# A two-layer attention and ffn block on one core: seams between stages, head, and who makes the low parts

## The chip, the cores and the metric
One core of a Trainium2 chip runs the whole program. The metric is the device time of one execution in microseconds (us); the time given for a kernel is the median of its runs.

## The reference, cut to what matters
Two layers, each a gated attention mixer and a convolutional ffn, with an rms norm ahead of each part and the residual added behind it (512 tokens, width 1024, float32):

```python
for l in range(2):
    h = rms_norm(x, g_pre_mix[l])
    m = hybrid_mixer(h, positions, w_in[l], ...)   # q, k, v, gates = h @ w_in; rope; two attentions
    x = x + rms_norm(m, g_post_mix[l])             # m = (g_a * (o_nsa @ w_a) + g_b * (o_sb @ w_b)) @ w_out
    h = rms_norm(x, g_pre_ffn[l])
    f = conv_ffn(h, w_up[l], conv_w[l], conv_b[l], w_down[l])
    x = x + rms_norm(f, g_post_ffn[l])
```

## The kernel before, in words
Everything lies feature-major, [128, 8, 512] for width 1024. The weights stream through three raw buffers `wraw` in chunks of 512 KB, by transfers on SyncE's queue (L73), in the order of a list made at the start. ScalarE casts a chunk to its high part `whi` (L94), and VectorE (DVE) or GpSimd, as the list says, subtracts it to get the low part `wlo` (L95); both have two buffers. Chunks that are kept for six tiles have both parts in one tile, `wh`. A projection (`gemm`, L362) makes three matmuls for each of the eight feature tiles of a chunk: `h_hi` with `whi`, `h_lo` with `whi`, `h_hi` with `wlo`.

The norm isn't applied to h. `chain` makes h = x * gain in two parts (`h_hi` on ScalarE, L431, `h_lo` on DVE, L432), and sums the squares of x (ScalarE L435, GpSimd L439); a matmul with ones (L445) sums them over the features, and `rstd_of` (ScalarE L213 and L401, DVE L402 to L404) makes `r2` = 1 / rms, which multiplies the projection later. Ahead of that, when a part has ended, the chain adds the normed part to x: another matmul with ones (L415) on `acc` (mixer) or `f_acc` (ffn), the sums of squares of the part that GpSimd gathers tile by tile (L455).

So that TensorE has work at the seam between two parts, tokens are done by halves. The last tiles of a part run the second half while the chain of the first half runs as a side job; then `head_first` runs the first six tiles (`HEAD`) of the next projection on the first half, beside the chain of the second half, and `head_second` runs them on the second half. At the start of the program the chain has no part to add, and position tables (`rt_...`, sine and cosine, written to memory and read back as `cs_t`) are made beside `head_first`.

Behind the first six tiles of the mixer's input projection (`w_m`) come three chunks of `w_vn` (840, 840 and 560 columns, values, token-major), and `w_m` chunks 6 and 7. Key and query tiles are rotated on the way: a copy `rf`, its halves swapped by four transfers into `rs`, DVE products with `cs_t`. The rotated `kd` goes by transfers to `cstk`, which the matmuls of L671 read. The ffn's down projection `w_d` comes in pieces of 1024, 1024 and 768 columns for each output tile; the last three tiles (`TAIL_D`) are done by halves.

A scheduler with a cost model decides in which order each engine gets its instructions; each engine then runs its own in that order, and waits for the others by semaphores.

## Time and profile before

| | |
|---|---|
| time, median of 3 runs (lowest, highest) | 1701.48 us (1700.77, 1703.69) |
| span of the profiled execution | 1701.4 us |
| TensorE matmul busy (PE) | 1637.3 us, 96% |
| VectorE busy (DVE) | 1114.8 us, 66% |
| ScalarE busy (ACT) | 820.6 us, 48% |
| GpSimd busy (POOL) | 404.8 us, 24% |

The span is the time from the first to the last instruction of one execution, the one that was profiled; what lies around it is within the difference between the three runs. PE is TensorE's matmul stream, PEld its weight loads, which run beside it. An idle time in the timeline stands behind a row in brackets, with what ended it.

### The profile page before, as it was taken

Reading aid. Unit: us, or ns where it says so; the run is one execution under the profiler, and the core shown is the slowest. Engines: PE = TensorE matmul, PEld = TensorE weight load, DVE = VectorE, ACT = ScalarE, POOL = GpSimd, SP = SyncE. Lnnn points to the kernel's source line nnn. Section 1 sums busy time; section 2 is a strip of 40 time slices with the busy share of each in tenths; the row PEclk is TensorE's granted clock in tenths of the full one; section 3 lists DMA queues with packets and bytes.
Section 4 is the critical chain, followed back from the end, with each engine's and each line's share of the span. In section 5 each row is a group of like instructions: output and inputs, shape, how many; then the busy total and the mean of one; then the engine's idle time right before and its main releaser. Section 6 shows DMA issues by size and latency. Waiting matters only on the chain.

```text
span 1701.4 us, 23429 instructions
## 1 busy us (share of the span) xinstructions
PE 1637.3 (96%) x9010; PEld 1401.9 (82%) x9010; DVE 1114.8 (66%) x1595; ACT 820.6 (48%) x1358; POOL 404.8 (24%) x385
## 2 busy tenths in 40 slices
PE   7989999999989999999999999999999999999997
PEld 6878887778988888888888788877889988888896
DVE  8677665766478777722657667577675787776236
ACT  5445564545554444433544555464545454444233
POOL 4125453440240000001331354444203200000011
PEclk9999999999999999999999999999999999999998
DMA  4721112113312333233655211121142223333344
GB/s 163 194 88 50 50 38 63 50 52 135 124 63 75 99 99 98 88 99 102 186 171 146 68 50 51 38 62 50 50 163 85 75 87 99 100 98 91 97 126 138
DMA packets 56800, 159.98 MB, mean 94 GB/s; under 512 B 6512, under 2 KB 18288, under 8 KB 56432
## 3 DMA queue, kind: packets, MB, share of 16 engines
q1 hardware_dynamic: 51984, 147.92, 27.9%
q10 hardware_dynamic: 3552, 6.37, 1.1%
q0 software_dynamic: 1152, 4.19, 0.7%
q8 instruction: 71, 1.16, 0.3%
q14 instruction: 41, 0.34, 0.1%
HBM read 144.82 MB, written 4.72 MB: 88 GB/s over the span
## 4 chain that ended last, share of the span: by engine, by line
PE 82%; DVE 9%; ACT 4%; issue 2%; DMA 2%; POOL 1%; SPq 0%; ACTq 0%; DVEq 0%; POOLq 0%
PE bk L362 52%; PE f L362 16%; PE Z L362 4%; PE pv L362 3%; PE S L362 2%; PE tp L867 2%; DVE rs L425 1%; DVE x L426 1%; PE bk L671 1%; DMA cs_t<-rot 1%; DVE wlo L95 1%; DVE h_lo L432 1%; ACT whi L94 1%; ACT L220 0%; ACT gate L213 0%
## 5 line engine op out<-in xcount | busy, mean ns | idle before, releaser
L94 ACT CAST whi<-wraw 128x1024 fp32r<-128x1024 f32 (+3 forms) x241 | 246.2, 1022 | 351.8 <-PE bk L362 259.3
L95 DVE TENSOR_TENSOR wlo<-wraw,whi 128x1024 fp32r<-128x1024 f32 (+4 forms) x184 | 217.2, 1181 | 217.6 <-ACT whi L94 215.4
L362 PE MATMUL bk<-h_hi,whi 128*128 128x512 f32 (+1 forms) x768 | 288.6, 377 | 12.6 <-ACT whi L94 11.0
L362 PE MATMUL bk<-h_lo,whi 128*128 128x512 f32 (+1 forms) x768 | 290.2, 378 | 3.3 <-DVE h_lo L432 3.2
L362 PE MATMUL bk<-h_hi,wlo 128*128 128x512 f32 (+1 forms) x768 | 289.1, 377 | 4.1 <-DVE wlo L95 4.1
L95 POOL TENSOR_TENSOR wlo<-wraw,whi 128x1024 fp32r<-128x1024 f32 x57 | 141.3, 2480 | 231.2 <-ACT whi L94 187.2
L362 PE MATMUL f<-h_hi,whi 128*128 128x512 f32 x448 | 183.2, 409 | 4.8 <-DVE gate L734 2.0
L455 POOL TENSOR_TENSOR f_acc<-f_acc,sqm 128x256 f32<-128x256 f32 (+1 forms) x19 | 29.1, 1531 | 635.9 <-ACT sqm L454 635.8
L362 PEld LDWEIGHTS bk<-h_hi,whi 128*128 128x128 f32 x768 | 147.8, 193 | 37.6 <-ACT whi L94 11.0
L362 PE MATMUL f<-h_hi,wlo 128*128 128x512 f32 x448 | 178.7, 399 | 0.0
L362 PE MATMUL f<-h_lo,whi 128*128 128x512 f32 x448 | 178.5, 398 | 0.0
L362 PEld LDWEIGHTS bk<-h_hi,wlo 128*128 128x128 f32 x768 | 148.2, 193 | 30.5 <-DVE wlo L95 5.3
L362 PEld LDWEIGHTS bk<-h_lo,whi 128*128 128x128 f32 x768 | 148.3, 193 | 30.0 <-DVE h_lo L432 4.5
L362 PE MATMUL bk<-ah,wlo 128*128 128x256 f32 (+1 forms) x484 | 162.8, 336 | 4.0 <-DVE wlo L95 4.0
L362 PE MATMUL bk<-ah,whi 128*128 128x256 f32 (+1 forms) x484 | 161.1, 333 | 0.0
L362 PE MATMUL bk<-al,whi 128*128 128x256 f32 (+1 forms) x484 | 160.9, 332 | 0.0
L362 PEld LDWEIGHTS f<-h_hi,whi 128*128 128x128 f32 x448 | 85.7, 191 | 25.0 <-DVE sbz L713 4.1
L362 PEld LDWEIGHTS bk<-ah,wlo 128*128 128x128 f32 x484 | 92.5, 191 | 14.2 <-DVE wlo L95 5.0
L856 POOL TENSOR_TENSOR P<-P,st 128x256 f32<-128x256 f32 (+3 forms) x64 | 80.9, 1265 | 82.3 <-DVE st L854 53.1
L1150 DVE TENSOR_TENSOR cu<-bk,r 128x512 f32<-128x512 f32 x88 | 60.1, 686 | 61.2 <-PE bk L362 61.0
L362 PEld LDWEIGHTS f<-h_hi,wlo 128*128 128x128 f32 x448 | 85.5, 191 | 17.7
L362 PEld LDWEIGHTS bk<-ah,whi 128*128 128x128 f32 x484 | 92.6, 191 | 8.8
(227 smaller groups left out, 3456.5 us busy)
## 6 DMA issues: line engine op xcount, KB each, us to landing
wraw<-in_w_u SPq DMA_DIRECT2D x88, 512.0 KB, 3.5
wraw<-in_w_m SPq DMA_DIRECT2D x72, 512.0 KB, 3.3
wraw<-in_w_d SPq DMA_DIRECT2D x44, 512.0 KB, 3.5
wraw<-in_w_d SPq DMA_DIRECT2D x22, 384.0 KB, 3.1
wraw<-in_w_pr SPq DMA_DIRECT2D x16, 512.0 KB, 3.6
wraw<-in_w_o SPq DMA_DIRECT2D x16, 512.0 KB, 3.6
rs<-rf SPq DMA_DIRECT2D x56, 64.0 KB, 3.6
x<-in_xT ACTq DMA_DIRECT2D x4, 512.0 KB, 10.4
```

What stands on the lines that cost most here:

```text
L94: self.nc.scalar.copy(hi[:, c], raw[:, c])
L95: eng.tensor_sub(lo[:, c], raw[:, c], hi.bitcast(F)[:, c])
L362: nc.tensor.matmul(o, a, b, start=first, stop=last, skip_group_check=True)
L425: eng.tensor_mul(t, mt(k), r)
L426: eng.tensor_add(xk, xk, t)
L432: nc.vector.scalar_tensor_tensor(h_lo[:, k, tr], xk, g, h_hi.bitcast(F)[:, k, tr], op0=OP.mult, op1=OP.subtract)
L455: nc.gpsimd.tensor_add(acc, acc, q)
L671: nc.tensor.matmul(cps[v][:64, :65], cw[:, v * 1024 + s * 64:v * 1024 + s * 64 + 64], cstk[:, v, s:s + 513:8], start=(s == 0), stop=(s == 15))
L856: nc.gpsimd.tensor_mul(pv, pv, st[:, None, 2:4, None].to_broadcast([128, self.i + 1, 2, 128]))
L867: nc.tensor.transpose(tp[:, b * 128:(b + 1) * 128], self.P[:, (c + b) * 128:(c + b + 1) * 128], ident)
L1150: nc.vector.tensor_mul(u, b, r2)
```

## The change
It has five parts. (1) At the head x is transferred by SyncE, in four contiguous parts between the first weight chunks (x is kept by token halves, [128, 2, 8, 256]), the first `vec` by ScalarE's queue, and 48 matmuls of a constant tile run first on TensorE. (2) Where the chain has no part to add, the squares come behind all the h's. (3) The matmul on the sum of squares of the first half (`r2_of`) isn't issued at the end of the chain but after the third tile (`LATE` = 2) of `head_first`, and the last sum goes into `r2` itself. (4) The low parts of the second and third `w_vn` chunk, of `w_m` chunks 6 and 7, and of the second piece of the last three second-half `w_d` tiles are made on GpSimd, in both layers. (5) Comments are gone, so that lines are numbered anew.

```diff
-            it(w_vn[l, :, c:c + n], n)
-        it(w_m[l, 6])
-        it(w_m[l, 7])
+            it(w_vn[l, :, c:c + n], n, eng=nc.gpsimd if c else nc.vector)
+        it(w_m[l, 6], eng=nc.gpsimd)
+        it(w_m[l, 7], eng=nc.gpsimd)
...
-        for i in dts:
+        for j, i in enumerate(dts):
             k0 = 0
             for n in DCH:
-                it(w_d[l, i, :, k0 * 128:(k0 + n) * 128], n * 128)
+                it(w_d[l, i, :, k0 * 128:(k0 + n) * 128], n * 128, eng=nc.gpsimd if j >= 8 and k0 == 8 else nc.vector)
...
-    nc.sync.dma_start(vecs[0], vec[0])
+    nc.scalar.dma_start(vecs[0], vec[0])
     open_x()
-    load_x(xT, HALVES[:1])
+    load_x(xT, nc.sync, ((0, 0),))
+    W.prefetch(1)
+    load_x(xT, nc.sync, ((0, 1),))
+    W.prefetch(2)
+    load_x(xT, nc.sync, ((1, 0), (1, 1)))
     W.prefetch()
-    load_x(xT, HALVES[1:])
...
+        def square(k):
+            nonlocal sacc
+            q = tp_.tile([128, HT], F, name=nm("sq"), tag="sq", bufs=3)[:, :w]
+            nc.scalar.activation(q, x[:, hf, k], AF.Square)
+            to = r2[:, tr] if k == KD - 1 and late is not None else q
+            if sacc is not None:
+                nc.gpsimd.tensor_add(to, q, sacc)
+            sacc = to
+
+        def r2_of(behind=None):
+            s = fbank("ms")
+            op = nc.tensor.matmul(s[:, :w], ones, sacc, start=True, stop=True)
+            if behind is not None:
+                after(op, behind)
+            rstd_of(s[:, :w], r2[:, tr])
...
-        s = fbank("ms")
-        nc.tensor.matmul(s[:, :w], ones, sacc, start=True, stop=True)
-        rstd_of(s[:, :w], r2[:, tr])
-        yield
+        if post is None:
+            for k in range(KD):
+                square(k)
+                if k % 2 == 1:
+                    yield
+        if late is None:
+            r2_of()
+            yield
+        else:
+            late.append(r2_of)
...
             W.ensure(min(W.n_got + 1, W.n_got - 1 + HEAD - 1 - i))
+            if i == LATE:
+                while late:
+                    late.pop(0)(last_mm[0])
...
-                drain(chain(HALVES[0], pre=g_pre))
+                warm = fbank("f")
+                for _ in range(48):
+                    mm(warm[:, :128], nones, nones, True, True)
+                drain(chain(HALVES[0], pre=g_pre, late=late))
```

Three places show what the scheduler makes of it. First TensorE, where the mixer of layer 0 ends and the ffn begins. `bk_555` (in the changed kernel `bk_553`) is the bank of the ffn's first tile, `bk_557` (`bk_555`) that of the third. Before, around the two matmuls with ones:

```order
L362 MATMUL bk_555_4568<-h_hi_97,wlo55_4338 128x256
L362 MATMUL bk_555_4568<-h_hi_97,whi55_4337 128x256
L445 MATMUL ms_548_4521<-sq_547_4506,ones_87 128x256
L362 MATMUL bk_555_4568<-h_lo_98,whi55_4337 128x256
L362 MATMUL bk_555_4568<-h_hi_97,wlo55_4338 128x256
...
L362 MATMUL bk_557_4570<-h_hi_97,wh57_567_4616 128x256 x2
L415 MATMUL ms_561_4586<-acc_464_3692,ones_87 128x256
L362 MATMUL bk_557_4570<-h_lo_98,wh57_567_4616 128x256
```

And in the changed kernel, with the bank of the fourth tile, `bk_556`, at the end:

```order
L366 MATMUL bk_553_4608<-h_lo_99,whi55_4387 128x256
L366 MATMUL bk_553_4608<-h_hi_98,wlo55_4388 128x256
L421 MATMUL ms_559_4626<-acc_465_3742,ones_87 128x256
L366 MATMUL bk_553_4608<-h_hi_98,whi55_4387 128x256
L366 MATMUL bk_553_4608<-h_lo_99,whi55_4387 128x256
...
L366 MATMUL bk_555_4610<-h_hi_98,wh57_565_4656 128x256
L438 MATMUL ms_576_4751<-r2_89,ones_87 128x256
L366 MATMUL bk_556_4611<-h_hi_98,wh58_570_4701 128x256
```

The matmul on the squares of the first half has gone from the first tile to the end of the third, and the one on `acc` has come from within the third to near the end of the first, two matmuls behind the old place of the other; in layer 1 it stands six behind. On GpSimd the sum that it reads stands, as before, directly behind the last sum of squares.

Second ScalarE, at the start of the program; before:

```order
L435 ACTIVATE sq_21_147<-x_2_71 128x256
L431 ACTIVATE h_hi_97<-x_2_71,vec0_65 128x256
L304 DMA rt_inv_231<-in_inv 128x2
L94 CAST whi0_122<-wraw0_74 128x512 x2
L305 DMA rt_pi_226<-in_pos 128x512
L431 ACTIVATE h_hi_97<-x_2_71,vec0_65 128x256 x4
```

In the changed kernel:

```order
L430 ACTIVATE sq_20_202<-x_2_71 128x256
L430 ACTIVATE sq_21_204<-x_2_71 128x256
L430 ACTIVATE sq_22_207<-x_2_71 128x256
L454 ACTIVATE h_hi_98<-x_2_71,vec0_65 128x256 x4
L308 DMA rt_pi_263<-in_pos 128x512
L430 ACTIVATE sq_23_210<-x_2_71 128x256
L95 CAST whi0_123<-wraw0_73 128x512 x2
```

Three squares now stand first, and the transfer of the positions ahead of the first cast of weights.

Third DVE in the same place, from the low part of the first chunk on; the changed kernel alone, since before it the cast to `rt_ang` stood behind the second chunk's low part and four more `h_lo`:

```order
L96 TENSOR_TENSOR wlo0_124<-wraw0_73,whi0_123 128x512 x2
L455 SCALAR_TENSOR_TENSOR h_lo_99<-x_2_71,vec0_65,h_hi_98 128x256 x3
L310 CAST rt_ang_264<-rt_pi_263 128x512
L455 SCALAR_TENSOR_TENSOR h_lo_99<-x_2_71,vec0_65,h_hi_98 128x256
L311 TENSOR_SCALAR rt_ang_264<-rt_ang_264,rt_inv_268 128x512
L96 TENSOR_TENSOR wlo1_132<-wraw1_76,whi1_131 128x1024
```

The cast of the positions has moved ahead of the last `h_lo` of the first half and of the second chunk's low part.

## Rows read from the trace of the kernel before

**Rows 1.** Busy time on the page: engine, us (share of the span), instructions.

```profile
PE 1637.3 (96%) x9010; PEld 1401.9 (82%) x9010; DVE 1114.8 (66%) x1595; ACT 820.6 (48%) x1358; POOL 404.8 (24%) x385
```

**Rows 2.** Waits of TensorE: us in total, times, longest us.

```profile
PE bk L362 <- ACT whi L94: 11.6, 4, 11.0
PE bk L362 <- DVE wlo L95: 10.0, 7, 3.1
PE ms L445 <- POOL sq L439: 7.7, 2, 3.8
PE bk L671 <- DMA cstk<-kd: 4.6, 1, 4.6
PE bk L362 <- DVE h_lo L432: 3.2, 4, 1.0
```

**Rows 3.** Stretches: us, busy (instructions) by engine, granted clock, transfers.

```profile
core 0: us, PE busy (x) PEld busy (x) DVE busy (x) ACT busy (x) POOL busy (x), PEclk, DMA share, GB/s
482.00:486.00 4.00, 4.00 (x19) 3.87 (x18) 2.89 (x5) 2.25 (x4) 1.07 (x1) 0.50 0.78 251
...
490.00:494.00 4.00, 4.00 (x35) 4.00 (x35) 3.46 (x10) 1.89 (x6) 0.00 (x0) 1.00 0.00 0
```

**Rows 4.** Timeline of the head: start, us, engine, line, operation, idle before.

```profile
7.77 0.51 ACT L431 ACTIVATE h_hi<-x,vec 128x256 fp32r<-128x256 f32 x1 [5.68 <-issue]
8.19 0.40 ACT L435 ACTIVATE sq<-x 128x256 f32<-128x256 f32 x1
...
10.30 1.12 ACT L94 CAST whi<-wraw 128x512 fp32r<-128x512 f32 x2
...
10.96 0.58 PE L362 MATMUL bk<-h_hi,whi 128*128 128x256 f32 x1 [10.96 <-ACT whi L94]
```

**Rows 5.** Transfers: queue, count, KB each, median us from issue to landing.

```profile
wraw<-in_w_m SPq DMA_DIRECT2D x72, 512.0 KB, 3.3
...
x<-in_xT ACTq DMA_DIRECT2D x4, 512.0 KB, 10.4
...
cstk<-kd SPq DMA_DIRECT2D x16, 64.0 KB, 2.0
...
rt_pi<-in_pos ACTq DMA_DIRECT2D x1, 256.0 KB, 6.8
```

**Rows 6.** Timeline of TensorE, two waits of layer 0.

```profile
64.56 0.60 PE L362 MATMUL bk<-wlo,h_hi 128*128 128x280 f32 x1 [1.92 <-DVE wlo L95]
...
89.75 0.45 PE L671 MATMUL bk<-cstk,cw 128*64 128x65 f32 x2 [4.57 <-DMA cstk<-kd]
```

**Rows 7.** Timeline of GpSimd and DVE, a low part and rotations.

```profile
80.97 2.44 POOL L95 TENSOR_TENSOR wlo<-wraw,whi 128x1024 fp32r<-128x1024 f32 x1 [3.03 <-ACT whi L94]
81.07 2.88 DVE L571 TENSOR_TENSOR rt<-rf,cs_t 128x512 f32<-128x512 f32 x1
...
87.85 0.68 DVE L571 TENSOR_TENSOR rt<-rf,cs_t 128x512 f32<-128x512 f32 x1
```

**Rows 8.** Timeline of TensorE and GpSimd where layer 0's mixer ends.

```profile
477.34 0.28 PE L362 MATMUL bk<-h_hi,whi 128*128 128x256 f32 x1
...
480.17 1.23 POOL L439 TENSOR_TENSOR sq<-sq,sq 128x256 f32<-128x256 f32 x1 [1.16 <-ACT sq L435]
481.36 1.71 POOL L455 TENSOR_TENSOR acc<-acc,sqm 128x256 f32<-128x256 f32 x1
...
481.45 1.22 PE L445 MATMUL ms<-sq,ones 128*128 128x256 f32 x2 [3.83 <-POOL sq L439]
```

**Rows 9.** Timeline of TensorE, tail of `w_d`, layer 0: first and last of three waits.

```profile
836.46 0.39 PE L362 MATMUL bk<-ah,wlo 128*128 128x256 f32 x1 [1.16 <-DVE wlo L95]
...
844.80 0.39 PE L362 MATMUL bk<-ah,wlo 128*128 128x256 f32 x1 [1.84 <-DVE wlo L95]
```

**Rows 10.** Timeline of ScalarE, tail of `w_d`, layer 1.

```profile
1655.18 1.05 ACT L94 CAST whi<-wraw 128x1024 fp32r<-128x1024 f32 x1 [1.11 <-PE bk L362]
```

**Rows 11.** Timeline of TensorE and SyncE's queue, `w_m` chunks 6 and 7, layer 1.

```profile
908.76 0.50 PE L362 MATMUL bk<-h_hi,wlo 128*128 128x512 f32 x1 [0.89 <-DVE wlo L95]
917.58 0.70 PE L362 MATMUL bk<-h_hi,wlo 128*128 128x512 f32 x1 [3.08 <-DVE wlo L95]
...
923.30 2.41 SPq L611 DMA_DIRECT2D cstk<-kd  x4
...
929.84 0.43 PE L671 MATMUL bk<-cstk,cw 128*64 128x65 f32 x2
```

More of the change, by code (lines that the diff above doesn't have):

```diff
@@ L33 @@
 TAIL_D = 3
+LATE = 2
 ALL = slice(0, T)
@@ L66, in __init__, with prefetch @@
         self.n_got = 0
-    def prefetch(self):
-        while self.n_dma < min(len(self.items), self.n_split + 3):
+    def prefetch(self, ahead=3):
+        while self.n_dma < min(len(self.items), self.n_split + ahead):
             i = self.n_dma
@@ L206, in after @@
                           mybir.DependencyInfo(mybir.DependencyClass.NoSync, mybir.DependencyReason.DATA),
-                          reason="order of the tables")
+                          reason="order of issue")
     def act(out_, in_, fn, **kw):
@@ L233, in open_x, with load_x @@
         xp = x_ctx.enter_context(pool("xp", side="right"))
-        x = xp.tile([128, KD, T], F, name=nm("x"))
-    def load_x(src, trs=HALVES, eng=None):
-        for tr in trs:
-            for c in range(2):
-                (eng or nc.scalar).dma_start(x[:, 4 * c:4 * c + 4, tr], src[:, 4 * c:4 * c + 4, tr])
+        x = xp.tile([128, 2, KD, HT], F, name=nm("x"))
+    def load_x(src, eng, parts=((0, 0), (0, 1), (1, 0), (1, 1))):
+        for h, c in parts:
+            eng.dma_start(x[:, h, 4 * c:4 * c + 4], src[:, h, 4 * c:4 * c + 4])
     load_table(AF.Exp)
     vecs = [cp.tile([128, VEC_W], F, name=f"vec{l}") for l in range(DEPTH)]
-    nc.sync.dma_start(vecs[0], vec[0])
+    nc.scalar.dma_start(vecs[0], vec[0])
     open_x()
-    load_x(xT, HALVES[:1])
+    load_x(xT, nc.sync, ((0, 0),))
[3 more added lines that the diff above has]
+    load_x(xT, nc.sync, ((1, 0), (1, 1)))
     W.prefetch()
-    load_x(xT, HALVES[1:])
     for l in range(1, DEPTH):
@@ L260, in run_kernel @@
     nones = cp.tile([128, 128], FR, name="nones")
+    nc.vector.tensor_scalar(nones, ones, -float(D), None, op0=OP.mult)
     negl = cp.tile([128, 128], FR, name="negl")
@@ L291, in constants @@
             nc.vector.tensor_copy(identb, ident)
-            nc.vector.tensor_scalar(nones, ones, -float(D), None, op0=OP.mult)
             nc.vector.tensor_copy(negl, scr)
@@ L345, in run_kernel @@
     n_tmp = 0
+    last_mm = [None]
     @contextmanager
@@ L361, in mm @@
     def mm(o, a, b, first, last):
-        nc.tensor.matmul(o, a, b, start=first, stop=last, skip_group_check=True)
+        return nc.tensor.matmul(o, a, b, start=first, stop=last, skip_group_check=True)
     def fbank(name):
@@ L404, in rstd_of, with chain @@
         nc.vector.scalar_tensor_tensor(r, q, 1.5, r, op0=OP.add, op1=OP.mult)
-    def chain(tr, post=None, pre=None, store=None, shared=False):
+    def chain(tr, post=None, pre=None, store=None, shared=False, late=None):
         w = tr.stop - tr.start
+        hf = tr.start // HT
         if post is not None:
@@ L433, in chain @@
                                                op1=OP.subtract)
-                q = tp_.tile([128, HT], F, name=nm("sq"), tag="sq", bufs=3)[:, :w]
-                nc.scalar.activation(q, xk, AF.Square)
-                if k == 0:
-                    sacc = q
-                else:
-                    nc.gpsimd.tensor_add(q, q, sacc)
-                    sacc = q
+                if post is not None:
+                    square(k)
             yield
@@ L443, in chain @@
             return
-        s = fbank("ms")
-        nc.tensor.matmul(s[:, :w], ones, sacc, start=True, stop=True)
-        rstd_of(s[:, :w], r2[:, tr])
-        yield
+        if post is None:
+            for k in range(KD):
+                square(k)
+                if k % 2 == 1:
[5 more added lines that the diff above has]
+            late.append(r2_of)
     def square_acc(src, acc, k):
@@ L455, in square_acc, with head_first @@
             nc.gpsimd.tensor_add(acc, acc, q)
-    def head_first(banks, side):
+    def head_first(banks, side, late):
         kept = []
@@ L479, in run_kernel @@
     side_next = None
+    late = []
     for l in range(DEPTH):
@@ L525, in run_kernel @@
                 side = side_next
-            kept = head_first(banks, side)
+            kept = head_first(banks, side, late)
         f_ctx.close()
@@ L1055, in run_kernel @@
         open_x()
-        load_x(xT if l == 0 else xmid, eng=nc.gpsimd)
+        load_x(xT if l == 0 else xmid, nc.gpsimd)
         with temps(5) as yt:
@@ L1114, in run_kernel @@
                 post = lambda tr: (lambda k: at(m_t, k)[:, tr], (acc[:, tr],))
-                side = Side((chain(HALVES[0], post=post(HALVES[0]), pre=g_pre2), 0.5))
+                side = Side((chain(HALVES[0], post=post(HALVES[0]), pre=g_pre2, late=late), 0.5))
                 for i, m in enumerate([6, 7, 2, 3, 4, 5]):
@@ L1130, in run_kernel @@
             side = Side((chain(HALVES[1], post=post(HALVES[1]), pre=g_pre2), 0.5))
-            for i in head_second(banks, head_first(banks, side)):
+            for i in head_second(banks, head_first(banks, side, late)):
                 pass
@@ L1193, in run_kernel @@
             dst = out if last else xmid
-            side = Side((chain(HALVES[0], post=post(HALVES[0]), pre=pre, store=dst), 0.4))
+            side = Side((chain(HALVES[0], post=post(HALVES[0]), pre=pre, store=dst, late=late), 0.4))
             for m in range(n0, 8):
```

14 lines of the change are left out of this document (7 added, 7 removed).

## The prediction

> **What bounds the kernel now.** The view of busy time comes first: TensorE is busy for 1637.3 of the 1701.4 us of the span [rows 1]. The other 64 us are the pool from which any edit outside TensorE can win. The view of waits, for TensorE, splits that pool [rows 2]: 11.6 us for high parts (11.0 of it the start of the program), 10.0 us in seven waits for low parts, 7.7 us in two waits of a mean-square matmul for a sum on GpSimd, 4.6 us for the `cstk` transfer, 3.2 us for `h_lo`. The change addresses all of these but the transfer. The timeline around each wait says what ends it, and so what stands behind it; the order of the instructions (shown with the change) says whether the changed program still waits there. One cost is not in the view of waits: after a stall the clock falls. In the 4 us after the stall at 481 TensorE gets 19 matmuls of 256 columns through at a granted clock of 0.50 (the lower level, 1.2 GHz), in the 4 us from 490, at 1.00, 35 [rows 3]: 0.21 against 0.114 us each. About 26 of them go at the slow pace, so a long stall costs some 2.5 us more than its own length.
>
> All sums below are made against the profiled execution, whose span is 1701.4 us; the median of the three runs shown is 1701.48, so the two can be taken as one.
>
> **1. The head.** `h_hi` begins at 7.77 us, the first cast of weights at 10.30, TensorE at 10.96 [rows 4]. The reason is that four parts of x share the transfer engines with the first chunks: an x transfer of 512 KB takes 10.4 us to land, where a weight transfer of the same size takes 3.3 [rows 5]. In the change the first x part is alone ahead of everything. Taking 3.3 us from an issue at about 1.2, it is there at 4.5. ScalarE then has three squares (0.40 by the nearest square, less as they overlap; I take 1.1 in all), four `h_hi` (1.7), one square (0.35) and half a cast (0.55) in its row ahead of the first matmul: 4.5 + 3.7 = 8.2 us. TensorE starts 2.7 us earlier, and the 48 constant matmuls, which have nothing to wait for but `nones`, have it at full clock, worth up to another 2.5.
>
> It does not keep this. DVE's row now has the cast of `rt_pi` ahead of the last `h_lo` of the first half and of the second chunk's low part. That 256 KB transfer took 6.8 us to land [rows 5]; it is issued behind the four `h_hi`, at about 7.3, so it may land at 14.1, where DVE would otherwise be at 11. So TensorE's gain here is anything from 0 to 5. More important is where it goes. TensorE stands still at 89.75 us for 4.57 us, waiting for `cstk` [rows 6], which ends a chain of its own: position tables on DVE, sine on ScalarE, two transfers, the rotation, `kd`. A gain ahead of that point counts only as far as this chain is shorter. The chain starts 2.2 us earlier (first `h_lo` at about 6.1 instead of 8.31, the end of the first `h_hi`). The first `w_vn` low part and three small operations of `r2` move behind the tables: -2.3. Against it, `rt_pi` up to +3, and a cast (0.9) and a logarithm (0.4) stand ahead of the transfer of the tables on ScalarE: +1.3. Bounds -4.5 and +1, taken as -2.5.
>
> **2. Low parts to GpSimd, layer 0.** Waiting for the third `w_vn` low part costs 1.92 us [rows 6] and about 1.5 of clock. This goes, but TensorE only comes earlier to the wait at 89.75. Does the chain to `kd` get shorter? DVE is rid of 0.7 + 1.2 + 1.2 us of low parts ahead of `kd`. But a low part on GpSimd is not free for DVE. One ran from 80.97 for 2.44 us, and the DVE multiply which began 0.1 us behind it took 2.88 us instead of 0.68 [rows 7]: 2.2 us lost, where doing the low part itself costs DVE 1.2. The Trainium skill, page "SBUF — State Buffer", section "SBUF: two separate sides", gives the rule: DVE operations with two SBUF inputs and GpSimd operations take one shared port pair exclusively, for the whole instruction. The trace agrees, with the 2.88 us. By that rule alone each moved low part would cost DVE about 1 us net; without it, it would save 1.2. Three of them: bounds -3.5 and +3, taken as -0.5, since DVE idles in places in this stretch where a lock costs nothing. Parts 1 and 2 together: **-3** (-8 to +4).
>
> **3. The mean-square matmul, mix to ffn, both layers.** The wait is 3.83 us, from 477.6 to 481.45, and it ends just after GpSimd's last sum of squares, 480.17 + 1.23 = 481.40 [rows 8]. In the order after, this matmul is gone from the place. But the other mean-square matmul, the one on `acc` that begins the second half's chain, has come up from the third tile to the end of the first, and it waits for GpSimd as well: for the sum that stands directly behind the old one, 481.36 + 1.71 = 483.07 [rows 8]. Nothing ahead of it on GpSimd or ScalarE is moved. So the stall ends 1.67 us later, and TensorE gets done meanwhile only what stands between the two places in its row, 2 matmuls in layer 0 and 6 in layer 1, at 0.12 us: +1.4 and +1.0. The drop of the clock behind the stall stays. **+2.4**, bounds -1 (some of the sum comes earlier) and +4 (the stall also costs 0.6 us more at the slow clock). The matmul that was moved costs nothing in its new place, three tiles ahead of its first reader.
>
> **4. Tail of `w_d`.** In layer 0 TensorE waits for three DVE low parts, from 1.16 us (836.46) to 1.84 (844.80), with one of 0.97 between [rows 9]: 4.0. DVE is behind there, with chain operations between the low parts; with three fewer low parts on it the next ones come some 3.7 us earlier in its row. A low part on GpSimd has its own bound. The cast before it can start when the chunk before the last is done, so the low part is ready 1.04 + 2.44 = 3.5 us after, while TensorE needs 24 x 0.114 = 2.7 for the chunk between and 0.24 more until it wants the low part: a wait of 0.4 to 0.6 for each of three chunks. Layer 0: -4.0 + 1.5 = **-2.5** (-4 to +1). In layer 1 the cast of such a chunk, at 1655.18, was followed by a DVE low part without a wait of TensorE [rows 10]; there the same edit costs **+1.2** (0 to +1.6).
>
> **5. ffn to mix.** The half-0 `r2` moves out of the tail into the head of the next layer, and puts three DVE operations of 0.43 into the second half's chain, for whose `h_lo` TensorE already waits (1.9 of the 3.2 us in rows 2): at most +1.3, at least 0, taken as **+0.8**.
>
> **6. Layer 1, `w_vn` and two `w_m` chunks.** Waits of 0.89 and 3.08 us [rows 11], and about 1.6 for the clock after the longer: 5.6. These low parts wait in DVE's row behind rotations which wait for transfers; GpSimd, idle here, starts them as soon as the cast is done. But TensorE then meets `cstk`: its transfers were issued from 923.30 over 2.41 us and took 2.0 to land [rows 5, 11], so it was there at about 927.7, and TensorE came at 929.84 without a wait. 2.1 of the 5.6 are sure, the rest only if `kd` comes earlier too, which is part 2's question again. **-3.3** (-5.6 to 0).
>
> The x layout, squares behind the h's, and `nones` made earlier cost nothing that I can find: squares wait on GpSimd, idle until 9 us here.
>
> **Sum**: -3 + 2.4 - 2.5 + 1.2 + 0.8 - 3.3 = -4.4, so 1701.4 - 4.4 = **1697.0 us**, -0.26%.
>
> **Rivals.**
> (a) *The seams are really cured.* If the acc sum came earlier than traced, both stalls would fall: 2 x (3.83 + 2.5) = 12.7 less, in place of +2.4. 1697.0 - 15 = 1682. The order speaks against it; only a sum on GpSimd that is ready by 478 would do it. Chance 0.06.
> (b) *GpSimd locks DVE out: slower.* Each moved low part falls beside a two-input DVE operation and costs 2.2 us instead of 1.2. Then `kd` is 3 us later in both layers. In layer 0 that takes the head's 2.5 (0 in place of -3), in layer 1 `kd` at 925 makes `cstk` land at 930.7, 0.9 behind the arrival of before (+0.9 in place of -3.3), in the tail DVE is as late as before with GpSimd's own 1.5 on top (+1.5 in place of -2.5), and the chain of part 5 +1.3. Sum +1 + 0.9 + 1.5 + 2.4 + 1.2 + 1.3 = +8: 1709. It decides from the point where `kd` in layer 1 comes more than 2.1 us later than now. For it: the 2.88 us. It is the rule of the Trainium skill's page "SBUF — State Buffer", "SBUF: two separate sides", taken at every low part; the trace shows it at one. Against: DVE idles 2.8 us just ahead in layer 1, where one low part fits. Chance 0.18.
> (c) *Given back*: head and low parts win what I say at their own places, but both waits for `cstk` take it: parts 1, 2 and 6 are worth -2.5 together, the rest +1.9. 1700.8. For it: a transfer chain bounds both places. Chance 0.28.
> (d) My forecast with its own range, 1692 to 1700: chance 0.48.
>
> **How the numbers follow.** About 0.2% (3.4 us) is what a measurement of this kernel can tell from no change: below 1698.1 is faster, above 1704.9 slower. Faster: (a) and some two thirds of (d), plus a little of (c): 0.06 + 0.40 + 0.04 = 0.5. Slower: most of (b), 0.15. Same: the rest, 0.35. To leave out no more than 2 in 10 the range goes from 1689 (parts 1 to 6 near their good ends, but with the seams as they are) to 1706, half way into (b).
>
> **What will show it.** In the timeline after: TensorE's first weight matmul at about 8 us, with constant matmuls ahead; a wait of 3.5 us or more of `ms<-acc` near 480 and 1315 (no wait there would be rival a); a wait at `cstk`'s matmul in layer 0 of 3 to 8 us, and a new one, 0 to 3 us, in layer 1; waits for GpSimd low parts of some 0.5 us, three in each tail; DVE multiplies of 2.5 us and more beside GpSimd low parts. What makes it wrong most easily is `kd`: it is priced by one locked operation, and decides parts 2 and 6.

## The result and the profile after

The changed kernel takes 1709.16 us (median of 5 runs, 1705.86 to 1718.72) where the kernel before took 1703.69 beside it (5 runs). The ratio on record is 1.0058, with an interval of 1.0036 to 1.0080; it is not the quotient of these two medians, which is 1.0032 (5.5 us). By either it is slower; 1697.0 was forecast.

Both kernels vary from run to run by more than the forecast gain (the kernel before from 1694.5 to 1706.5 over all its runs here), and the traced execution of the changed kernel is the longest of its five: a span of 1716.8 us at a mean granted clock of 0.979, where before had 1701.4 at 0.984. So the trace shows 15.4 us, the ratio 0.58% (9.9 us). Where the 15.4 lie is read from the start of one and the same matmul in both traces; each row is what a stage took longer than before (the first matmul on `cstk`, the first `S`, the output projection, the first and last `w_d` matmul of a layer, the end).

| stage | after - before, us | forecast |
|---|---|---|
| start to the first `S` of layer 0 (parts 1, 2) | +0.5 | -3 |
| attention, layer 0 (not changed) | +3.7 | 0 |
| output projection, seam, `w_u`, layer 0 (part 3) | +1.0 | +1.4 |
| `w_d`, layer 0 (part 4) | +1.9 | -2.5 |
| ffn to mix, `w_m` and `w_vn`, to `cstk`, layer 1 (parts 5, 6) | +3.4 | -2.5 |
| attention, layer 1 (not changed) | +1.3 | 0 |
| output projection, seam, `w_u`, layer 1 (part 3) | +0.3 | +1.0 |
| `w_d` and end, layer 1 (part 4) | +3.3 | +1.2 |

The changed places sum to +10.4, near the ratio's 9.9. That can be luck in part: a stage of a single trace moves by 4 us and more with no change to its code, as the kernels below show, so a stage is read safely only where several kernels repeat it. The other 5.0 lie in attention code whose order is nearly the same (of some 350 rows of DVE in each layer, at most 5 stand elsewhere). In layer 0 it is the clock, as these stretches of the changed kernel (first line) and of the kernel before (second) show; the columns are as in rows 3.

```profile
290.00:300.00 10.00, 10.00 (x33) 7.75 (x33) 8.74 (x7) 4.88 (x5) 4.94 (x7) 0.66 0.28 79
```

```profile
290.00:300.00 10.00, 10.00 (x55) 8.63 (x55) 8.31 (x7) 5.30 (x5) 4.94 (x9) 1.00 0.29 82
```

TensorE counts as busy throughout in both; it gets 33 matmuls through at 0.66 and 55 at 1.00. Part of this stretch of the changed kernel is at the lower level, none of the other. The same code gives other times in the kernels below: in five of them the stage takes 0.1 to 0.6 us less than before, in six 0.9 to 2.7 us more. So it is put down to the execution and not to the change.

A steadier measure is the span of a run times its mean granted clock, averaged over the runs of a kernel. (The clock is on record to 0.001, and the product leaves out what a wait costs by lowering the clock.) The kernel before has 1672 and the changed one 1682.0, with a standard error of some 0.5, so about 10 us more.

Busy time on the page of the changed kernel, answering to rows 1:

```profile
PE 1655.0 (96%) x9058; PEld 1415.3 (82%) x9058; DVE 1108.3 (65%) x1581; ACT 820.5 (48%) x1359; POOL 434.0 (25%) x399
```

TensorE is busy 17.7 us longer: 10.5 of it are the constant matmuls, the rest work at the slow pace. DVE lost 6.5 us, GpSimd gained 29.2 for 14 more low parts. The waits of TensorE, answering to rows 2:

```profile
PE ms L421 <- POOL acc L479: 6.0, 2, 3.3
PE bk L366 <- POOL wlo L96: 6.0, 8, 2.2
PE bk L366 <- DVE h_lo L455: 6.0, 5, 1.7
PE bk L366 <- DVE wlo L96: 5.8, 5, 2.3
...
PE bk L366 <- DVE kd L659: 2.2, 1, 2.2
PE bk L702 <- DMA rs<-rf: 2.1, 1, 2.1
```

The 10.0 us for low parts have become 5.8 on DVE and 6.0 on GpSimd, with 1.4 more on GpSimd for the bank `f`; `h_lo` has grown from 3.2 to 6.0; the seams keep 6.0 of 7.7, now on `acc`. Five places explain it.

**The head.** Timelines of the changed kernel: TensorE, then ScalarE, then DVE.

```profile
1.90 10.51 PE L366 MATMUL f<-nones 128*128 128x128 f32 x48 [1.90 <-DVE nones L264]
12.20 0.52 PE L366 MATMUL bk<-h_hi,whi 128*128 128x256 f32 x1
```

```profile
7.99 1.12 ACT L95 CAST whi<-wraw 128x512 fp32r<-128x512 f32 x2
```

```profile
13.50 0.63 DVE L310 CAST rt_ang<-rt_pi 128x512 f32<-128x512 int32 x1 [1.87 <-DMA rt_pi<-in_pos]
```

The cast begins at 7.99, 0.3 later than the forecast had it, but the 48 constant matmuls take 0.215 us each and hold TensorE to 12.2, later than before (10.96 in rows 4). DVE waits for `rt_pi` until 13.50, near the bound that the prediction gave (14.1).

**A lock ahead of `cstk`, layer 0.** GpSimd and DVE, then TensorE's wait that answers to rows 6:

```profile
82.91 2.94 POOL L96 TENSOR_TENSOR wlo<-wraw,whi 128x1024 fp32r<-128x1024 f32 x1 [2.23 <-ACT whi L95]
82.93 3.48 DVE L602 TENSOR_TENSOR rt<-rf,cs_t 128x512 f32<-128x512 f32 x2
...
89.45 2.80 PE L702 MATMUL bk<-cstk,cw 128*64 128x65 f32 x22 [2.09 <-DMA rs<-rf]
```

Two DVE multiplies take 3.48 us, where one alone takes 0.68 [rows 7]. TensorE comes 2.2 us later to the wait than before and leaves it 0.3 us earlier. (The releaser is a neighbour in the queue; the matmul reads `cstk`.)

**The seam.** GpSimd and TensorE where layer 0's mixer ends, answering to rows 8:

```profile
485.56 1.70 POOL L479 TENSOR_TENSOR acc<-acc,sqm 128x256 f32<-128x256 f32 x1
...
483.55 0.39 PE L366 MATMUL bk<-h_lo,whi 128*128 128x256 f32 x1 [1.72 <-DVE h_lo L455]
...
487.32 1.22 PE L421 MATMUL ms<-acc,ones 128*128 128x256 f32 x2 [3.27 <-POOL acc L479]
```

The wait for the sum of squares has gone; that for the `acc` sum directly behind it has come, ending 0.06 us after the sum. Ahead of it TensorE now also waits 1.72 us for `h_lo`, which one of the matmuls between the two places reads. In layer 1 it is the same, with 1.72 and 2.76; these two waits for `h_lo`, 3.4 us, are why it has grown.

**The tail of `w_d`, layer 0.** GpSimd, DVE and TensorE:

```profile
829.72 2.40 POOL L96 TENSOR_TENSOR wlo<-wraw,whi 128x1024 fp32r<-128x1024 f32 x1 [6.29 <-ACT whi L95]
832.08 0.73 POOL L479 TENSOR_TENSOR f_acc<-f_acc,sqm 128x256 f32<-128x256 f32 x1
...
836.11 1.23 DVE L96 TENSOR_TENSOR wlo<-wraw,whi 128x1024 fp32r<-128x1024 f32 x1 [2.48 <-ACT whi L95]
837.25 0.42 DVE L406 TENSOR_SCALAR rv<-ms 128x256 f32<-128x256 f32 x1
...
838.69 2.95 DVE L448 TENSOR_TENSOR rs<-f_t,rstd 128x256 f32<-128x256 f32 x2
838.70 2.67 POOL L96 TENSOR_TENSOR wlo<-wraw,whi 128x1024 fp32r<-128x1024 f32 x1 [5.89 <-ACT whi L95]
...
850.68 0.39 PE L366 MATMUL bk<-ah,wlo 128*128 128x256 f32 x1 [2.34 <-DVE wlo L96]
```

The sum of squares that the chain needs (`f_acc`) stands on GpSimd behind a low part; the chain's first DVE operation, `rv`, comes at 837.25; before it came at 828.11, so 3.9 us later once the 5.2 by which the stage starts later are taken off. (Some of that is order: the sum ends at 832.81, and its matmul now stands in TensorE's row at 835.14.) Then a low part and the pair `rs` begin 0.01 us apart, and the pair takes 2.95. Six waits of TensorE in this tail sum to 5.2 us, the longest 2.34; before there were three of 4.0 in all [rows 9].

**Layer 1, up to `cstk`.** ScalarE with its queue, GpSimd and DVE, then TensorE's waits:

```profile
891.21 0.90 ACT L95 CAST whi<-wraw 128x840 fp32r<-128x840 f32 x1
892.01 0.41 ACT L405 ACTIVATE rq<-r 128x256 f32<-128x256 f32 x1
892.19 1.99 POOL L96 TENSOR_TENSOR wlo<-wraw,whi 128x840 fp32r<-128x840 f32 x1 [4.12 <-ACT whi L95]
892.46 2.01 DVE L407 TENSOR_TENSOR rq<-rv,rq 128x256 f32<-128x256 f32 x1 [2.21 <-ACT rq L405]
...
895.87 0.44 ACTq L570 DMA_DIRECT2D cs_t<-rot  x1
```

```profile
908.68 0.40 PE L366 MATMUL bk<-whi,h_hi 128*128 128x280 f32 x1 [2.18 <-DVE kd L659]
...
926.35 0.50 PE L366 MATMUL bk<-h_hi,wlo 128*128 128x512 f32 x1 [1.21 <-POOL wlo L96]
...
940.35 4.84 PE L702 MATMUL bk<-cstk,cw 128*64 128x65 f32 x39 [1.60 <-DMA cstk<-kd]
```

A small DVE operation (`rq`, 0.42 where no low part runs beside it) takes 2.01 beside the low part that was moved to GpSimd. From it `r` is made, until 894.93, and only then ScalarE issues the transfer of the tables `cs_t`, at 895.87. In the kernel before:

```profile
885.54 0.44 ACTq L539 DMA_DIRECT2D cs_t<-rot  x1
```

That is 10.3 us, of which 7.1 are the late start of the stage, so 3.2 are lost here. The lock has up to 1.6 of them (2.01 against 0.42). But 2.2 of the 3.2 stay when the low parts are back on DVE (below): ScalarE's own `rq` now stands behind a cast (891.21), since the squares matmul of the first half comes later (part 5). Behind it come `kd`, for which TensorE now waits 2.18, and `cstk`, for which it waits 1.60. The 0.89 and 3.08 of rows 11 have gone; with waits for low parts of 0.54, 1.21 and 1.38 five others, 6.9 us in all, have come.

### The profile page after: what moved, and what is told of

Its sections match the earlier page's. It is cut to its first block, busy times and chain, and to the rows that moved or that the text cites. A ratio compares the mean times of both kernels' runs of the same rounds, so it can differ in the third digit from the quotient of the medians.

```text
span 1716.8 us, 23524 instructions
## 1 busy us (share of the span) xinstructions
PE 1655.0 (96%) x9058; PEld 1415.3 (82%) x9058; DVE 1108.3 (65%) x1581; ACT 820.5 (48%) x1359; POOL 434.0 (25%) x399
## 3 DMA queue, kind: packets, MB, share of 16 engines
q8 instruction: 71, 1.16, 0.3%
## 4 chain that ended last, share of the span: by engine, by line
PE 80%; DVE 8%; ACT 4%; DMA 3%; issue 2%; POOL 2%; SPq 1%; ACTq 0%; DVEq 0%; POOLq 0%
PE bk L366 49%; PE f L366 17%; PE Z L366 5%; PE pv L366 3%; PE S L366 2%; PE tp L898 2%; DVE rs L448 1%; ACT whi L95 1%; DVE x L449 1%; PE bk L702 1%; DMA rs<-rf 1%; DVE wlo L96 1%; DMA pew<-in_pew 1%; POOL wlo L96 1%; DMA cs_t<-rot 1%
## 5 line engine op out<-in xcount | busy, mean ns | idle before, releaser
L96 DVE TENSOR_TENSOR wlo<-wraw,whi 128x1024 fp32r<-128x1024 f32 (+3 forms) x170 | 201.6, 1187 | 226.4 <-ACT whi L95 224.4
L96 POOL TENSOR_TENSOR wlo<-wraw,whi 128x1024 fp32r<-128x1024 f32 (+1 forms) x71 | 177.4, 2499 | 265.0 <-ACT whi L95 247.7
L366 PEld LDWEIGHTS bk<-al,whi 128*128 128x128 f32 x484 | 92.5, 191 | 8.7
```

The costliest lines, as they stand in the source:

```text
L96: eng.tensor_sub(lo[:, c], raw[:, c], hi.bitcast(F)[:, c])
L366: return nc.tensor.matmul(o, a, b, start=first, stop=last, skip_group_check=True)
```

## The experiments

Each is an edit of the changed kernel, alone or on top of others as said. A ratio is against the kernel before on the same chip. "From ... to ..." is a stage of the table above in the profiled execution, against before.

**Without the 48 constant matmuls.**

```diff
-                warm = fbank("f")
-                for _ in range(48):
-                    mm(warm[:, :128], nones, nones, True, True)
```

> The changed kernel without the 48 constant matmuls. Theory (they hold TensorE until 12.2 us, when the first weights were ready at about 8.5, but the cstk chain on DVE and ScalarE ends at 89.4 either way): the first weight matmul comes at 8.5 us, TensorE waits some 3 us longer at cstk, the wait ends within 1 us of 89.45, and the whole time stays within 1.5 us of the changed kernel's 1709. Rival (what TensorE wins at the start it keeps): the wait at cstk ends 3 us earlier and the time is about 1706.

1710.04 us, 1.0058 [1.0040, 1.0076]: no change of the total. But TensorE begins at 9.00, and the place is not the same:

```profile
85.54 7.84 PE L699 MATMUL bk<-cstk,cw 128*64 128x65 f32 x64 [2.67 <-DMA cstk<-kd]
```

The wait for `cstk` ends 3.9 us earlier than in the changed kernel, so it is not fixed by `rt_pi`; layer 0 is ahead of before by 4.3 us at the first `S`. Counting a stretch at the lower clock half, it is 0.8 there: most of the lead is a stretch at the lower level that this run has not had yet. What is left goes within the spread of the runs. Nor are the 3.9 us the constant matmuls' price: the kernel with the seams undone, below, has all 48 of them and begins on `cstk` at 85.92. So the constant matmuls hold back the first weight matmuls, but they are not what made the kernel slower, and no run shows what they cost at `cstk`.

**Low parts of `w_vn` and `w_m` back on DVE.**

```diff
-            it(w_vn[l, :, c:c + n], n, eng=nc.gpsimd if c else nc.vector)
-        it(w_m[l, 6], eng=nc.gpsimd)
-        it(w_m[l, 7], eng=nc.gpsimd)
+            it(w_vn[l, :, c:c + n], n)
+        it(w_m[l, 6])
+        it(w_m[l, 7])
```

> The changed kernel with the low parts of the w_vn chunks and of w_m chunks 6 and 7 back on DVE in both layers. Theory (on GpSimd they lock DVE out and come later than TensorE wants them): the three GpSimd waits and the cstk wait of layer 1 (0.5 + 1.2 + 1.4 + 1.6 us) go, the two DVE waits of before (0.9 + 3.1) come back, layer 0 is as before; together -1 to -4 us against 1709. Rival (the lock costs nothing, the moved low parts were a gain): 3 to 5 us slower than 1709.

1708.15 us, 1.0044 [1.0027, 1.0061]. From layer 0's last `w_d` to layer 1's `cstk` it takes 0.7 less than before, where the changed kernel took 3.4 more: 4.1 won. DVE's `rq` is at its own length again:

```profile
884.49 0.42 DVE L407 TENSOR_TENSOR rq<-rv,rq 128x256 f32<-128x256 f32 x1
```

The lock on `rq` is shown by this row. That part 6 is a loss is not, since neither the total nor the stage settles it. The two intervals overlap, and span times clock differs by 2.0 us with a standard error of 1.1. The stage does not repeat:

| layer 0's last `w_d` to layer 1's `cstk` | after - before, us |
|---|---|
| low parts on GpSimd, squares matmul late (changed kernel and four below) | +1.9 to +3.4 |
| low parts on GpSimd, squares matmul not late (seams undone, below) | -0.7 |
| low parts on DVE, squares matmul late: this run; 18 wide matmuls | -0.7; -1.6 |
| the same: three mended; with the head of before; 12 wide matmuls | +5.2; +5.7; +5.1 |

In the last three TensorE waits 4.6 to 5.2 us for DVE's low part of `w_m` chunk 7 and goes at the lower clock for 6.8 us about its end; in the two of the row above it waits 1.1 and 1.5 us, and no stretch is at the lower clock.

**Low parts of the `w_d` tails back on DVE.**

```diff
-                it(..., n * 128, eng=nc.gpsimd if j >= 8 and k0 == 8 else nc.vector)
+                it(..., n * 128)
```

> The changed kernel with the low parts of the w_d tail back on DVE. Theory (in the tail a GpSimd low part is late by itself and makes DVE late): the waits of layer 0's tail fall from 4.7 us to the 4.0 of before, those of layer 1 from 2.9 to 0: -3 to -5 us, about 1705. Rival (the tail gains in layer 0, and the loss lies elsewhere): 0 to +2 us.

1706.94 us, 1.0034 [1.0017, 1.0050]. Layer 0's `w_d` takes 1.9 less than before (changed: 1.9 more), layer 1's and the end 0.3 more (changed: 3.3 more): 3.8 and 3.0 won. This repeats: in the five later kernels without these low parts on GpSimd the two stages take 0.4 and 0.1 to 0.2 us less than before, and in the five kernels with all three there (changed, and four others) 1.9 to 3.3 and 3.3 to 3.6 more. Span times clock falls from 1682.0 to 1677.5. The waits of layer 0 are those of before, 1.16, 0.95 and 1.84, and the pair `rs` beside no low part takes its own time:

```profile
829.95 0.76 DVE L448 TENSOR_TENSOR rs<-f_t,rstd 128x256 f32<-128x256 f32 x2
```

**Only two of the three tail tiles on GpSimd**, so that the first low part no longer stands ahead of the `f_acc` sum.

```diff
-... eng=nc.gpsimd if j >= 8 and k0 == 8 else nc.vector)
+... eng=nc.gpsimd if j >= 9 and k0 == 8 else nc.vector)
```

> The changed kernel with only two of the three tail low parts of w_d on GpSimd, the first (three tiles from the end) back on DVE. Theory (half of the tail's loss is that GpSimd's sum f_acc, which the chain of the first half waits for, stands behind the first of these low parts): the chain's first matmul in layer 0 comes some 2 to 4 us earlier against its tile, the DVE low-part waits of 0.9 and 2.3 us in layer 0 shrink below 1.5 together; 1706 to 1708. Rival (it is DVE locked out beside GpSimd low parts): those waits stay, and the time stays at 1709 within 1 us.

1714.64 us, 1.0076 [1.0062, 1.0090]: neither theory. The chain does start earlier (`rv` of layer 1 at 1672.12 instead of 1683.95, 3.9 once the stage's own shift is out), which confirms the queue behind the low part, with the order that follows from it. All the kernels agree: counted from the layer's first `w_d` matmul, `rv` comes at 107.6 to 107.9 us in the five with all three tiles on GpSimd and at 103.6 to 103.7 in the other eight. But now the chain meets the next low part. GpSimd, the last of DVE's operations beside it, TensorE:

```profile
1676.97 6.25 POOL L96 TENSOR_TENSOR wlo<-wraw,whi 128x1024 fp32r<-128x1024 f32 x1 [6.71 <-ACT whi L95]
...
1680.07 0.95 DVE L96 TENSOR_TENSOR wlo<-wraw,whi 128x768 fp32r<-128x768 f32 x1
...
1683.27 0.58 PE L366 MATMUL bk<-ah,wlo 128*128 128x256 f32 x1 [3.96 <-POOL wlo L96]
```

The same subtraction that takes 2.4 us takes 6.25. DVE ran two-input operations without a gap from 1674.24 to 1681.02 at their usual length (0.75 for a pair); the low part ended 2.2 us after, a subtraction's length. Here DVE shut GpSimd out. The Trainium skill, page "SBUF — State Buffer", section "SBUF: two separate sides", says that whichever of the two starts first has the shared pair for its whole instruction. The trace agrees, from either side: 2.2 us lost on DVE in the changed kernel's tail, 3.9 on GpSimd here. Behind the wait of 3.96 us TensorE's clock is at the lower level for 6.8 us, and all five runs of this kernel have a low mean clock (0.979 to 0.982).

**The second half's chain held back at the seam**, three steps, its matmul on `acc` tied behind the projection's last.

```diff
+            for _ in range(hold):
+                yield
...
-                nc.tensor.matmul(s[:, :w], ones, a, start=i == 0, stop=i == len(accs) - 1)
+                op = nc.tensor.matmul(s[:, :w], ones, a, start=i == 0, stop=i == len(accs) - 1)
+                if hold and i == 0:
+                    after(op, last_mm[0])
...
-            side = Side((chain(HALVES[1], post=post(HALVES[1]), pre=g_pre2), 0.5))
+            side = Side((chain(HALVES[1], post=post(HALVES[1]), pre=g_pre2, hold=3), 0.5))
```

> The changed kernel with the chain of the second half held back by three steps at the seam from mixer to ffn, and its first matmul (on acc) tied behind the matmul of ffn tile 1 or 2 that was issued last. Theory (the matmul on acc took the place of the one that was moved, and waits for the sum directly behind): with both out of the first tile the stalls of 3.3 and 2.8 us go, and the low clock behind them: 8 to 11 us less, about 1699 to 1701. Rival (the stall only moves on, to h_lo of the second half, which is now later): within 2 us of 1709.

1704.30 us, 1.0019 [1.0008, 1.0029], the largest gain of any single edit, though less than the 8 to 11 us expected.

```profile
483.85 0.59 PE L423 MATMUL ms<-acc,ones 128*128 128x256 f32 x2
```

No wait, since the sum was there at 482.49. The seam stages take 3.3 and 4.3 less than before (changed: 1.0 and 0.3 more): 4.3 and 4.6 won. That is the 3 us wait and some of the clock behind it. It repeats: in all six kernels with the chain held back these stages take 3.3 and 3.1 to 4.3 less than before.

**The squares matmul back at the end of the chain**, at the seams (part 3 undone).

```diff
-... chain(HALVES[0], post=post(HALVES[0]), pre=g_pre2, late=late), 0.5))
+... chain(HALVES[0], post=post(HALVES[0]), pre=g_pre2), 0.5))
...
-... chain(HALVES[0], post=post(HALVES[0]), pre=pre, store=dst, late=late), 0.4))
+... chain(HALVES[0], post=post(HALVES[0]), pre=pre, store=dst), 0.4))
```

> The changed kernel with the squares matmul back at the end of the chain at the seams (at the start of the program it stays late). Theory (the edit only exchanges one stall for another that ends 1.7 us later): the stalls of the squares matmul come back at both seams from mixer to ffn, each with 3.8 us, and the time is 1 to 3 us less than the changed kernel's 1709, 1706 to 1708. Rival (the edit alone, with its three DVE operations at the head of layer 1, is what made the kernel slower): 5 us less or more.

1716.66 us, 1.0101 [1.0080, 1.0122]: missed. At the seams it does what it should; the old wait is back and the stages take +0.1 and -0.3 against before, 0.9 and 0.6 less than in the changed kernel:

```profile
479.03 1.22 PE L438 MATMUL ms<-sq,ones 128*128 128x256 f32 x2 [3.95 <-POOL sq L433]
```

The loss is elsewhere: layer 1's attention takes 9.4 us longer than before, 7.8 of it from the first `Z` on. There the scheduler gave DVE another order: of 352 rows about half stand elsewhere than before, in each other kernel at most 3. So the total says nothing of part 3; only the stages do.

The edit also puts the squares matmul back at the seam from ffn to mix, so it undoes part 5, and the low parts stay on GpSimd. Between the two layers the kernel is at -0.7 where the changed one is at +3.4, with no wait for `kd` or `cstk`:

```profile
886.04 0.44 ACTq L570 DMA_DIRECT2D cs_t<-rot  x1
```

From layer 0's last `w_d` matmul this is 31.6 us, where before had 31.2, the changed kernel 34.4, and the run with these low parts on DVE 33.4. So in this chain the moved squares matmul costs more than the moved low parts do. (Other rows of the stage are in another order too, so this is one sign and not a proof.)

**The three losses mended together**: no constant matmuls, all the moved low parts on DVE, the chain held back. The edits are those above.

```diff
+            it(w_vn[l, :, c:c + n], n)
...
+            side = Side((chain(HALVES[1], ..., hold=3), 0.5))
```

> The changed kernel without the constant matmuls, with all low parts back on DVE, and with the second half's chain held back at the seam from mixer to ffn; x by halves, its first transfers, the late squares matmul stay. Theory (the losses of the parts add up, each at its own place): by the single runs 2 to 5 us each from low parts in the tail, low parts of w_vn and the seam, so 1694 to 1699, below the kernel before (1701.6). Rival (a gain at one place is taken back at the next wait): 1701 or more.

1695.96 us, 0.9966 [0.9951, 0.9981]: as expected, and faster than before. Span times clock, 1671.1, is 10.9 below the changed kernel. What the single edits won, in hundredths of a per cent of before (0, 14, 24 and 39 from 58), would leave -19; -34 was measured.

**The same with the head of before** (x by ScalarE's queue in the old order, squares beside the h's).

```diff
-    load_x(xT, nc.sync, ((0, 0),))
-    W.prefetch(1)
...
+    load_x(xT, nc.scalar, ((0, 0), (0, 1)))
```

> The first run of this group (no constant matmuls, low parts on DVE, seam held) with the head of the kernel before as well: x on ScalarE's queue, vec first on SyncE's, squares between the h's, the squares matmul of the start not late. Theory (x ahead of the weights is worth something once the constant matmuls are gone): 1 to 4 us slower than that run. Rival (the wait for cstk swallows the head): the same within 1 us.

1698.11 us, 0.9983 [0.9971, 0.9994]; 2.2 us more than with the new head, and the wait for `cstk` is 4.27 again, ending at 86.37 instead of 83.99. The new head without its constant matmuls (order of x, squares behind the h's, squares matmul late) is worth about 2 us, near the 2.5 of part 1. The two intervals overlap, so the size is not settled.

**Wide constant matmuls** on top of the three mended losses: 12 of 512 columns, then 18.

```diff
-                for _ in range(48):
-                    mm(warm[:, :128], nones, nones, True, True)
+                wide = nones[:, None, :].to_broadcast([128, 4, 128])
+                for _ in range(12):
+                    mm(warm.rearrange("p (a b) -> p a b", a=4), nones, wide, True, True)
```

> The run before with 12 constant matmuls of 512 columns at the head, which should end at about 7 us, ahead of the first weights. Theory (the 48 narrow ones failed only because they ended too late): TensorE's first weight matmuls go at 0.12 us instead of 0.21 and the first wait matmuls of ones come 1 to 2.5 us earlier; the whole time 0 to 2 us less than the run before. Rival (constant matmuls ahead of a pause don't bring the clock up): the granted clock rises at about 14 to 15 us as without them, and the time is the same within 1 us.

1693.20 us, 0.9952 [0.9935, 0.9968], the fastest median of all. Timeline of TensorE, with one row of DVE:

```profile
1.90 4.87 PE L366 MATMUL f<-nones 128*128 128x512 f32 x12 [1.90 <-DVE nones L264]
8.85 0.38 PE L366 MATMUL bk<-h_hi,whi 128*128 128x256 f32 x1 [2.08 <-ACT whi L95]
...
81.75 7.84 PE L707 MATMUL bk<-cstk,cw 128*64 128x65 f32 x64 [0.78 <-DMA cstk<-kd]
...
906.79 2.81 DVE L607 TENSOR_TENSOR rt<-rf,cs_t 128x512 f32<-128x512 f32 x1 [3.41 <-DMA rs<-rf]
...
911.39 0.80 PE L366 MATMUL bk<-h_hi,wlo 128*128 128x512 f32 x1 [5.21 <-DVE wlo L96]
```

They are done by 6.8 us and delay nothing. But the pace that was expected of them did not come: from 10.1 to 16.5 us the weight matmuls still take some 0.21 us each or more, and the clock is at the lower level from 9.31 for 6.8 us. The median is 2.8 us below that without them, but the intervals overlap. Eighteen in place of twelve:

> The mended kernel with 18 instead of 12 wide constant matmuls, which fill most of the pause of 2.1 us ahead of the first weights. Theory (the clock fell at 9.3 us because of that pause): no low stretch in the head, the first 24 weight matmuls at 0.12 us, and 1 to 2.5 us less than 1693 at the cstk wait or none if that chain ends the wait. Rival (the clock falls all the same): head and time as with 12, within 1 us.

1694.28 us, 0.9965 [0.9951, 0.9979]. They last until 9.1, the first weight matmuls follow at 0.12 us each instead of 0.21, and nothing more is gained: TensorE then waits 2.01 us at 14.55 for what it outran. The low part for which the kernel with 12 waited 5.21 us comes sooner here, with the same code:

```profile
909.26 0.50 PE L366 MATMUL bk<-h_hi,wlo 128*128 128x512 f32 x1 [1.51 <-DVE wlo L96]
```

With 12, the DVE multiply ahead of it (906.79) began 0.1 us behind a low part on GpSimd and took 2.81 us; with 18 it takes 0.69 and DVE's low part begins 0.3 us ahead of the one on GpSimd. So the long wait is a matter of timing, and does not come merely from the low part being made on DVE.

**One low part on GpSimd**, where the kernel with 12 wide matmuls waits 5.21 us: `w_m` chunk 7 alone.

```diff
-        it(w_m[l, 7])
+        it(w_m[l, 7], eng=nc.gpsimd)
```

> The mended kernel with 12 wide constant matmuls (1693.2), and the low part of w_m chunk 7 alone on GpSimd, in both layers. Theory (one GpSimd low part that falls where DVE waits for a transfer takes TensorE's longest remaining wait, 5.2 us, without locking DVE for long): the wait in layer 1 falls below 2 us, the low clock behind it goes, 3 to 6 us less, 1687 to 1690. Rival (DVE and GpSimd lock each other out here too, and the cstk chain is as late as it was): no gain, within 1.5 us of 1693.

1693.42 us, 0.9966 [0.9950, 0.9982].

```profile
914.08 0.50 PE L366 MATMUL f<-h_hi,wlo 128*128 128x512 f32 x1 [0.95 <-POOL wlo L96]
```

The wait falls from 5.21 to 0.95, and the profiled execution is 5.4 us ahead of the former at layer 1's `cstk`; the time is no better within the intervals. The expected 1687 to 1690 was missed. The 18 wide matmuls reach the same stage time (-1.6 against -1.5) with this low part on DVE, so the trace of the kernel with 12 was an unlucky one to compare with. What the move is worth stays open.

## Why the prediction was wrong

Its sum was -4.4, where the changed places show +10.4. The step that is shown to have failed is part 4's price of a low part on GpSimd in the tail: only the low part's own lateness was counted, and the stages of layers 0 and 1, put at -2.5 and +1.2, took 1.9 and 3.3 more, which went when the low parts went back. For layer 1's start (parts 5 and 6) the forecast failed as well, but the runs do not settle which step of it. By its own parts:

1. **The head (part 1).** What failed here is that the constant matmuls "have nothing to wait for but `nones`": true, but TensorE's weight matmuls stand behind them. They were taken as over by 8.2 us; at 0.215 each they last until 12.2. The cast was nearly right (7.99), and so was `rt_pi`'s bound (13.50 against 14.1). What this cost at `cstk` no run shows: with the same head, and the low parts on GpSimd, five kernels come to the first `S` between 3.3 us earlier and 0.8 later than before. The run with the head of before gives the rest of part 1 about 2 us, where 2.5 was put.
2. **Low parts in layer 0 (part 2).** Taken as -0.5 between -3.5 and +3. Locks of 2.2 us were there, at 82.93 among other places. With parts 1 and 2 together the stage shows +0.5 for -3, inside the bounds given (-8 to +4). With these low parts back on DVE it shows -3.7, but a kernel with them on GpSimd shows -3.3, so their price is open.
3. **The seam (part 3).** Right in mechanism and sign: the wait went to the `acc` sum. It is 3.27 and 2.76 us, below the 3.5 or more asked for, because 1.72 of the standstill now counts as a wait for `h_lo`. Only the size was off: 1.0 and 0.3 in place of 1.4 and 1.0; undone, it gives 0.9 and 0.6. Rival (a), the cured seam, did not happen, but the chain held back shows what the cure is worth: 4.3 and 4.6 us against the changed kernel.
4. **The tail (part 4).** Wrong sign in layer 0: +1.9 for -2.5; in layer 1 +3.3 for +1.2. Low parts were put at 0.4 to 0.6 us of wait each, and they cost that (0.24 and 0.65). The missing steps are two: a GpSimd operation that the chain needs is queued behind the low part, and the chain then runs into the next one. Both were shown, the first by the earlier `rv` in the two-tile run and in every kernel without these low parts, the second by `rs` at 2.95 and 0.76 with and without a low part beside it.
5. **ffn to mix (part 5).** Too small, as far as is known. It counted three DVE operations on the way to `h_lo`, at most 1.3; the wait there is 1.23 in the changed kernel, less than the 1.9 of before. It did not count ScalarE's row, where a cast now stands ahead of `rq` and what is behind `rq` comes later. Without the move `cs_t` is issued 2.8 us earlier and the stage is 4.1 us shorter, in one trace whose other rows are in another order too.
6. **Layer 1 (part 6).** Parts 5 and 6 together show +3.4 for -2.5. The waits of rows 11 went as it said. GpSimd does start as soon as the cast is done, but takes some 2.4 us where DVE takes 1.2, a bound that part 4 priced and this part put at nothing: TensorE waits 0.54, 1.21 and 1.38 us for these low parts. And `kd` and `cstk` come later by more than the 2.1 us of slack that the prediction itself named as the point from which rival (b) decides. How much of that is the lock and how much part 5 stays open, since low parts back on DVE gave from -1.6 to +5.7.

**Rival (b)**, GpSimd locking DVE out, came nearest: the lock was there ahead of `cstk` in layer 0, in the tail and in layer 1. Its figure, 1709, is the time measured, but with some luck: its text puts the head at 0 where its sum has +1, and it was added to 1701.4, where the kernel before took 1703.69 beside the result. Its terms for the head, the first tail, the start of layer 1, the seams and the last tail (1, 1.5, 2.2, 2.4, 1.2) stand beside 0.5, 1.9, 3.4, 1.3 and 3.3 in the stages. The prediction had the 2.88 us row [rows 7], but priced the lock by DVE's busy time, about 1 us net for each low part, and took less than that. It did not ask which operation of which chain would be the one locked, nor what GpSimd itself had queued.

What is shown: the low parts in the tail cost 2 to 4 us in layer 0 and 3 to 4 in layer 1, in every kernel that has them there; the run without them is 0.24% (4 us) below the changed kernel, with an interval of some 3 us. The chain held back is worth 4.3 and 4.6 us by stages and 3.0 in all by span times clock, and the three edits together bring the kernel below the time of before. What is not: what the low parts of `w_vn` and `w_m` cost (0.14% by medians, which the intervals do not part from nothing), and how much lies in the 5.0 us of attention. In the run without the constant matmuls these stages take 0.1 and 0.2 less than before, so nothing shows a new cost of the code there.

## What to carry to other kernels

Before work is moved to GpSimd, list the two-input operations of DVE that will run beside it and the GpSimd operations that queue behind it; if one of them lies on a chain that TensorE waits for, the move can cost more than it takes off. Matmuls that warm the clock stand in TensorE's own row, so they must be over before the first operand comes. At a seam, see whether the wait is removed or handed to the next sum in the same queue; here holding the whole chain back was the cure, not moving one matmul. And a gain read in one stage of one trace has to be seen in a second kernel with the same code: here such a stage moved from -1.6 to +5.7 us.

## What was not expected of the hardware

A constant matmul of 128 columns takes as long as one of 256 does at the slow pace, 0.215 against 0.21 us; after 48 of them the weight matmuls went on at 0.21 until 14.65 us, then at 0.12. With 18 of 512 columns the pace was 0.12 from the first weight matmul to the next wait. In the head the records of the granted clock don't show this: over the constant matmuls they say 1.00.

```profile
2.00:12.00 10.00, 10.00 (x48) 10.00 (x48) 6.01 (x12) 6.94 (x18) 5.18 (x14) 1.00 0.97 334
```

The spread of this kernel's runs (1694.5 to 1706.5 for before, over all its runs here) goes with the mean granted clock: in the 23 runs beside the last experiments the span has a deviation of 3.2 us and the span times that clock 1.2; in 21 others it is 2.3 and 1.6. And an edit at the seams changed the scheduler's order through the whole attention of layer 1, for 9.4 us, so that a total can hide what a stage shows.
